# Fixed VectorE and ScalarE order in the first units of each up stage, put-off convolutions, partial products kept in PSUM

## The chip, the cores and the metric

The kernel runs on one core of one Trainium2 chip. The metric is device time in microseconds of one execution, as the median of several runs. TensorE is called PE below, VectorE DVE, ScalarE ACT, and SyncE's queue, which issues nearly all transfers here, SP.

## What is computed

A two-layer trunk over 1024 positions of width 1024, in float32. Layer 0 mixes positions with forgetting attention, layer 1 with a spatial gating MLP (SGU). After each mixer stands the same gated feed-forward block (FFN):

```python
def conv_gated_ffn(h, w_up, conv_w, conv_b, w_down):
    S = h.shape[1]
    a = h @ w_up                                   # 1024 x 1024 @ 1024 x 5632
    ap = jnp.pad(a, ((0, 0), (CONV_WIDTH - 1, 0), (0, 0)))
    acc = ap[:, 0:S] * conv_w[0]
    for j in range(1, CONV_WIDTH):
        acc = acc + ap[:, j:j + S] * conv_w[j]
    a = acc + conv_b
    g, val = jnp.split(a, 2, axis=-1)
    return (jax.nn.silu(g) * val) @ w_down
```

The SGU block begins with `z = gelu(h @ w_in + b_in)`, splits z into u and v, normalises v, mixes it over blocks of 128 positions, and multiplies the result by u ahead of its output product. Each block's input h is `modulate(rmsnorm(x, g), shift, scale)`; shift, scale and the residual's gate come from products of the conditioning vector c with `ada_w`.

## The kernel before

After the attention stage (`fox`) come three pairs of stages, each an `up` and a `down`: FFN of layer 0, SGU, FFN of layer 1. `up` multiplies the block's input by its first weight matrix, `down` the result by the second. Every float32 operand is split in two float32r parts, a rounded copy made by ACT (`put_hi`, line 1133) and the remainder made by DVE (`put_lo`, line 1136, drawn as line 1146 in the profile), and a product is three matmuls (`mm3`).

**Units.** `up` goes unit by unit: 22 in an FFN (128 columns of the gate half and 128 of the value half each), 16 in the SGU. The weights of a unit are two 128x1024 tiles, "g" and "v". Seen as 2x2 blocks, weights A11, A12, A21, A22 times operand blocks B11, B12, B21, B22 take eight block products. From unit 2 on seven products are used instead, by Winograd's form of Strassen's scheme: `p1` A11·B11, `p5` S1·T1, `p6` S2·T2, `p2` A12·B21, `p7` S3·T3, `p3` S4·B22, `p4` A22·T4, in this order. S1 to S4 are sums of weight blocks and T1 to T4 sums of operand blocks. One such product is 12 matmuls of 128x512 (`seven`, four groups of three). Units 0 and 1 are done in the plain form with eight products each, with T1 used in place of B12 (T1 is B12 less B11, so A11·B11 is added back); they need no S, and only B11, B21, T1 and B22. While they run, DVE and ACT have to make T2, T3, T4 and unit 2's sums.

**Units 0 and 1 before.** `half1(u)` makes A11·B11 and A21·B11 in banks a and Y, copies each to the right half R of the unit's output tile in SBUF (line 1386, ACT), and adds A12·B21 and A22·B21 on top (outputs 11 and 21, `post`). `half2` makes A11·T1 + A12·B22 and A21·T1 + A22·B22 in banks X and Y; `post` (line 1645) then adds the copy kept in R by a DVE `tensor_tensor`. The program runs half1(0), half1(1), T1 of both, then B22 of both.

**Weight slots.** The ring `owr` has four tiles of 128x2x1024, the raw weights come to a ring of four tiles `rawr`. In a steady unit, slot 0 takes A11/A12 (`put_a`), slot 1 the A22 of alternate units (`put_w`), slot 2 S3/S1 (`put_v`), slot 3 S2/S4 (`put_g`). `sums_u` makes the S blocks in place in the raw tiles with four DVE operations of 128x512. At the stage's start `start_up` puts g and v of unit 0 in slots 0 and 1, those of unit 1 in 2 and 3, between the last four products of the stage before.

**Operands.** `operands2` makes h in its second half of positions and from it T1, B22, T2, T3, T4. It spills x (four transfers on SP), takes the sum of squares by a matmul with ones, the inverse root on DVE (`norm_t`, `rsqrt`), multiplies a diagonal by ones on PE to spread it, scales x on DVE and ACT (`scale`), and writes the blocks (`put_ops`). `next_operands` hooks it to PE's groups of three matmuls with the numbers 7 and 14: its first part runs once eight groups of the stage have been issued, the rest after fifteen. `operands1` does the same for the first half of positions in the second-last part of `down`, one piece per step.

**After a product.** When both halves of an output are there, `post` in the FFN runs `conv` (line 1632 one ACT activation, line 1634 two DVE `scalar_tensor_tensor` of 128x1023 and 128x1022), SiLU on ACT for the gate half, and for the value half a DVE product; each second unit `store_y` makes four DVE sums and stores to memory. In the SGU, `post` applies GELU, and `natural` (lines 1725 to 1736) transposes v on PE, copies it with ACT, takes `bn_stats` on DVE and stores it.

**What sets the order.** PE's matmuls are chained by hand in program order (`mm`, `strict`). On the other engines a planner simulates the program and puts the instructions in an order by readiness; only between instructions chained by `vo` (DVE) or `ao` (ACT), while `ordered` is true, program order is kept. Before, `ordered` is true inside `operands2` alone. Each engine then runs its queue in that order. SP's queue is in order too: an issue that waits for a free tile holds those behind it.

**Other work in the stages.** `after(f)` of an FFN runs jobs of products with `ada_w` (line 262 four loads into the `rawr` ring, lines 270 and 272 eight DVE operations of 128x512): in the first FFN after units 4, 7, 10, 13, 16, 19. After unit 12, `sgu_tables` prepares tables for the SGU through the same ring.

Of the kernel before, what the change touches and what calls it, by code (L numbers as in the profile page):

```python
# [67 lines left out]
class Trunk:  # L68
# [1151 lines left out]
    def operands1(self, scales):  # L1220
# [7 lines left out]
        yield  # L1228
        next(n, None)
# [8 lines left out]
    def operands2(self, scales):  # L1238
        self.spill(1)
        self.xr.i = -1  # L1240
        self.ordered = True
        n = self.norm_t(1, *scales)
        next(n)
        self.ordered = False
        yield
        self.ordered = True
# [17 lines left out]
        self.put_ops("T2", [t2[:, k] for k in range(4)], second)  # L1264
        self.put_ops("T3", [h[:, L] for h in h2], lambda k: sub(h2[k][:, L], h2[k][:, R], h2[k][:, L]))
        for k in range(4):
            sub(h1[k][:, R], h1[k][:, R], t2[:, k])
        self.put_ops("T4", [h[:, R] for h in h1])
        self.ordered = False
# [26 lines left out]
    def sums_u(self, u):  # L1296
# [4 lines left out]
        self.tt(v[:, lo], g[:, lo], v[:, lo], ALU.subtract)  # L1301
        self.tt(g[:, lo], v[:, hi], g[:, lo], ALU.subtract)
        self.tt(g[:, hi], g[:, hi], g[:, lo], ALU.subtract)

# [30 lines left out]
    def up(self, n, src, post, after):  # L1335
# [45 lines left out]
        def half1(u):  # L1381
            a, x, y = bk[u]
            t = self.out_tiles(u)
            for c, (b, o) in enumerate(((a, "A11"), (y, "A21"))):
                self.seven(b, w[u][o], "B11", True)
                nc.scalar.copy(t[c][:, R], b)
            for b, o, q in ((a, "A12", "11"), (y, "A22", "21")):
                self.seven(b, w[u][o], "B21", False)
                post(u, q, b)

        def half2(u, o, j):
            a, x, y = bk[u]
            t = self.out_tiles(u)
            for c, b in enumerate((x, y)):
                self.seven(b, w[u][f"A{c + 1}{j}"], o, j == 1)
# [535 lines left out]
```

## Time and profile before

| | us |
|---|---|
| median of 3 runs | 2684.41 |
| lowest, highest | 2682.55, 2685.11 |
| the profiled execution | 2688.12 |
| its span, first to last instruction | 2686.3 |
| first up stage, first product | starts at 823.89 |
| SGU's up stage, first product | starts at 1487.02 |
| second FFN's up stage, first product | starts at 2012.73 |

The profiled execution took 1.8 us more than its span, and 3.7 us more than the median of the runs. A timeline row gives start, duration, engine, line, operation, output and inputs, the count of like instructions merged, and in brackets how long the engine had been idle before and which instruction ended that. A row of windows gives, for each engine, busy time and count in the stretch, then the TensorE clock granted (1.00 is full), the share of the DMA engines and the rate.

### The profile page before, as it was taken

To read this page: it belongs to the slowest core of one execution; us is meant where nothing else is said; L and a number is where in the kernel's file an instruction comes from. 1 tells how busy PE (TensorE), PEld (TensorE's weight loads), DVE (VectorE), ACT (ScalarE), POOL (GpSimd) and SP (SyncE) were. 2 spreads that over 40 slices of the span, in tenths; PEclk is the share of its full clock that TensorE was granted. 3 is DMA by queue.
4 is the path that set the end of the run, shared out by engine and by line. 5 is a ranking of instruction groups with operands and counts; after the bars stand their busy time and mean duration, and the time that the engine had idled before them with its cause. 6 is when DMAs were issued, how large, how long until landed. Compare 5 with 4: busy or idle time off the path is not lost.

```text
span 2686.3 us, 35378 instructions
## 1 busy us (share of the span) xinstructions
PE 2573.0 (96%) x12578; PEld 2186.3 (81%) x12578; DVE 2078.6 (77%) x3609; ACT 1463.1 (54%) x2321; POOL 171.5 (6%) x289
## 2 busy tenths in 40 slices
PE   6999999998989899999999999999998999999997
PEld 5988988898878788788888788888876888888886
DVE  7678777888667888888678766766888788877875
ACT  6347666777555545455446644654465545455444
POOL 1122222222100000000000000000000000000000
PEclk8999999999999999999999999999999999999999
DMA  7751111113232344546755346557552243337562
GB/s 232 232 185 56 56 52 56 56 52 99 89 105 74 121 131 140 182 141 200 244 160 171 105 153 190 190 181 275 159 177 72 96 148 116 118 104 286 158 200 91
DMA packets 316521, 379.46 MB, mean 141 GB/s; under 512 B 18872, under 2 KB 196152, under 8 KB 316344
## 3 DMA queue, kind: packets, MB, share of 16 engines
q1 hardware_dynamic: 316120, 377.14, 43.5%
q8 instruction: 99, 1.62, 0.3%
q14 instruction: 78, 0.64, 0.1%
q10 hardware_dynamic: 224, 0.06, 0.0%
HBM read 287.41 MB, written 89.72 MB: 140 GB/s over the span
## 4 chain that ended last, share of the span: by engine, by line
PE 78%; DVE 11%; ACT 4%; DMA 3%; issue 2%; SPq 1%; POOL 0%; DVEq 0%; ACTq 0%; POOLq 0%
PE bankX L104 20%; PE banka L104 17%; PE bankY L104 17%; PE pj L104 7%; PE ms L104 5%; PE o L104 3%; PE s L104 2%; PE ms L157 2%; PE op L104 2%; PE pv L104 1%; DVE ow L1146 1%; DVE hc L1146 1%; PE ms L1755 1%; DVE x L1146 1%; DVE x L1634 1%
## 5 line engine op out<-in xcount | busy, mean ns | idle before, releaser
L1133 ACT CAST ow<-rw 128x1024 fp32r<-128x1024 f32 (+1 forms) x438 | 398.7, 911 | 467.7 <-PE bankY L104 150.4
L1146 DVE TENSOR_TENSOR ow<-rw,ow 128x1024 fp32r<-128x1024 f32 (+1 forms) x438 | 457.0, 1045 | 173.9 <-ACT ow L1133 173.4
L104 PE MATMUL bankX<-hc,ow 128*128 128x512 f32 x1920 | 471.3, 394 | 18.5 <-DVE ow L1146 10.3
L104 PEld LDWEIGHTS bankX<-hc,ow 128*128 128x128 f32 x1920 | 361.1, 189 | 96.5 <-DVE ow L1146 11.9
L104 PE MATMUL banka<-hc,ow 128*128 128x512 f32 x1608 | 391.3, 392 | 1.7 <-DVE ow L1146 1.5
L104 PE MATMUL bankY<-hc,ow 128*128 128x512 f32 x1584 | 387.9, 391 | 0.8 <-DVE ow L1146 0.8
L104 PEld LDWEIGHTS banka<-hc,ow 128*128 128x128 f32 x1608 | 300.4, 188 | 64.4 <-DVE ow L1146 1.8
L104 PEld LDWEIGHTS bankY<-hc,ow 128*128 128x128 f32 x1584 | 296.1, 188 | 64.1 <-issue 1.9
L104 PE MATMUL pj<-x,h 128*128 128x384 f32 (+1 forms) x1536 | 316.6, 348 | 0.2 <-DVE x L119 0.2
L104 PEld LDWEIGHTS pj<-x,h 128*128 128x128 f32 x1536 | 272.6, 193 | 5.0 <-DVE x L119 0.5
L1634 DVE SCALAR_TENSOR_TENSOR x<-x,prm,x 128x1023 f32<-128x1023 f32 (+1 forms) x160 | 204.2, 1279 | 2.7 <-ACT x L1632 2.1
L104 PE MATMUL bankY<-ow 128*128 128x512 f32 x720 | 203.3, 390 | 0.2 <-DVE x L1150 0.2
L104 PE MATMUL banka<-ow 128*128 128x512 f32 x672 | 187.3, 391 | 0.5 <-DVE x L1150 0.5
L104 PEld LDWEIGHTS bankY<-ow 128*128 128x128 f32 x720 | 134.8, 188 | 28.4 <-DVE x L1150 0.6
L104 PE MATMUL bankX<-ow 128*128 128x512 f32 x588 | 156.1, 391 | 0.7 <-DVE ow L1146 0.5
L104 PEld LDWEIGHTS banka<-ow 128*128 128x128 f32 x672 | 125.8, 188 | 27.3 <-ACT x L1183 0.9
L104 PE MATMUL ms<-ow 128*128 128x512 f32 x546 | 139.9, 390 | 0.9 <-DVE pp L1146 0.9
L104 PE MATMUL pv<-pt,w 128*128 128x256 f32 (+1 forms) x640 | 119.8, 297 | 15.3 <-ACT pt L797 12.0
L119 DVE TENSOR_TENSOR pt<-ms,pt 128x512 fp32r<-128x512 f32 (+1 forms) x160 | 100.2, 632 | 40.3 <-ACT pt L797 38.8
L104 PEld LDWEIGHTS bankX<-ow 128*128 128x128 f32 x588 | 110.1, 188 | 25.0 <-DVE ow L1146 2.0
L104 PEld LDWEIGHTS ms<-ow 128*128 128x128 f32 x546 | 102.0, 188 | 23.7 <-DVE pp L1146 2.9
L797 ACT CAST pt<-ms 128x512 fp32r<-128x512 f32 (+1 forms) x160 | 85.4, 540 | 65.9 <-PE ms L157 55.5
(302 smaller groups left out, 3884.8 us busy)
## 6 DMA issues: line engine op xcount, KB each, us to landing
rw<-yd SPq DMA_DIRECT2D x210, 256.0 KB
rw<-in_ffn_w_up_dram SPq DMA_DIRECT2D x88, 512.0 KB
yd<-pp SPq DMA_DIRECT2D x60, 512.0 KB
rw<-in_ada_w_dram SPq DMA_DIRECT2D x48, 512.0 KB
rw<-in_ffn_w_down_dram SPq DMA_DIRECT2D x88, 256.0 KB
rw<-in_sgu_w_in_dram SPq DMA_DIRECT2D x32, 512.0 KB
yd<-x SPq DMA_DIRECT2D x30, 512.0 KB
fraw<-in_fox_w_in_dram SPq DMA_DIRECT2D x96, 128.0 KB
```

The source lines that it names most:

```text
L104: i = self.nc.tensor.matmul(out, lhsT, rhs, start=start, stop=stop, skip_group_check=self.strict)
L119: return (eng or self.nc.vector).tensor_tensor(lo, full, hi.bitcast(F32), op=ALU.subtract)
L157: i = self.nc.tensor.transpose(ps[: s.shape[1], j * P : (j + 1) * P], s, self.ident)
L797: nc.scalar.copy(pt[:, 0, :nb], ps[:, :nb])
L1133: return self.ao(self.nc.scalar.copy(t[:, 0], src))
L1146: return self.vo(self.nc.vector.tensor_tensor(out, a, b, op=op))
L1634: stt(o[:, j:], a[:, : S - j], w[2 - j], o[:, j:], op0=ALU.mult, op1=ALU.add)
L1755: k = nc.tensor.matmul(px[:, b * P : (b + 1) * P], vn[:, b, c * P : (c + 1) * P], sg[:, 0], start=True, stop=True)
```

## The change

In the three `up` stages:

- Units 0 and 1 are interleaved: A11·B11 of both, A12·B21 of both, then A21·B11 and A22·B21 of both (`first`). The partial product A11·B11 is copied by ACT to bank X and A21·B11 to bank a, where T1 and B22 products are accumulated on top. Outputs 12 and 22 are then complete in PSUM, and `post` copies them with ACT (GELU in the SGU) instead of adding with DVE.
- `start_up` therefore loads both units at once and puts g of both before v of both. Slots 1 and 2 change roles: S3/S1 to 1, A22 to 2.
- `operands2` is cut in four parts. The second ends after T2; T3, the four subtractions and T4 follow between B22 products, each ahead of or behind named weight work. `sums_u` is split into `sums_v` and `sums_g`.
- From the B22 products to the end of unit 3, `ordered` is true, so that DVE's `tt` and `conv` operations and ACT's `put_hi` and scale operations keep program order. ACT's copies, its SiLU and the first operation of `conv` are not chained.
- For units below 4, convolution, SiLU, product and store are put in the list `late`, and run one entry at a time at named points of units 2 to 4. In the SGU, `natural` of units 0 and 1 is put off in the same way.
- The operand hooks' numbers go from 7 and 14 to 3 and 10 in the first FFN (after four and eleven groups), and to 7 and 13 in the two other stages. `operands1` waits one step of `down` more ahead of its spreading matmul.
- The jobs of the first FFN run after units 5, 7, 9, 15, 17, 19.

```diff
     def operands2(self, scales):
         self.spill(1)
...
         self.put_ops("T2", [t2[:, k] for k in range(4)], second)
+        yield
         self.put_ops("T3", [h[:, L] for h in h2], lambda k: sub(h2[k][:, L], h2[k][:, R], h2[k][:, L]))
+        yield
         for k in range(4):
             sub(h1[k][:, R], h1[k][:, R], t2[:, k])
+        yield
         self.put_ops("T4", [h[:, R] for h in h1])
-        self.ordered = False
...
     def put_w(self, u):
-        self.put_u(u, "v", ("A22",), 1, u % 2)
+        self.put_u(u, "v", ("A22",), 2, u % 2)
     def put_v(self, u):
-        self.put_u(u, "v", ("S3", "S1"), 2)
+        self.put_u(u, "v", ("S3", "S1"), 1)
...
+        def first(us, c, j):
+            for u in us:
+                a, x, y = bk[u]
+                b = (a, y)[c]
+                self.out_tiles(u)
+                self.seven(b, w[u][f"A{c + 1}{j}"], ("B11", "B21")[j - 1], j == 1)
+                if j == 1:
+                    nc.scalar.copy((x, a)[c], b)
+                else:
+                    post(u, f"{c + 1}1", b)
+        def half2(u, o, j, cs=(0, 1)):
             a, x, y = bk[u]
+            for c in cs:
+                b = (x, a)[c]
+                self.seven(b, w[u][f"A{c + 1}{j}"], o, False)
                 if j == 2:
-                    post(u, f"{c + 1}2", b, t[c][:, R])
+                    post(u, f"{c + 1}2", b)
-        half1(0)
-        half1(1)
+        self.late = []
+        for c in range(2):
+            for j in (1, 2):
+                first((0, 1), c, j)
         half2(0, "T1", 1)
         half2(1, "T1", 1)
         self.load_u(2)
-        half2(0, "B22", 2)
+        self.ordered = True
+        self.put_w(2)
+        next(self.ops2)
+        half2(0, "B22", 2, (0,))
+        self.sums_v(2)
+        half2(0, "B22", 2, (1,))
         self.put_a(2)
-        self.put_w(2)
-        self.sums_u(2)
+        self.sums_g(2)
+        next(self.ops2)
+        half2(1, "B22", 2, (0,))
+        self.put_v(2)
+        next(self.ops2, None)
+        half2(1, "B22", 2, (1,))
+        self.put_g(2)
+        self.run_late()
         after(0)
-        half2(1, "B22", 2)
-        self.put_v(2)
-        self.put_g(2)
         after(1)
         for u in range(2, n):
-            more = u + 1 < n
+            more, early = u + 1 < n, u < 4
             p1(u)
             if more:
                 self.load_u(u + 1)
                 self.put_w(u + 1)
+            if u == 3:
+                self.run_late()
             p5(u)
+            self.run_late()
             p6(u)
             p2(u)
-            if more:
+            if early:
+                self.sums_v(u + 1)
+                if u == 2:
+                    self.run_late()
+                p7(u)
                 self.put_a(u + 1)
-                self.sums_u(u + 1)
-            p7(u)
-            if more:
+                self.sums_g(u + 1)
+                p3(u)
                 self.put_v(u + 1)
-            p3(u)
-            if more:
+                if u == 3:
+                    self.run_late()
+                p4(u)
                 self.put_g(u + 1)
-            p4(u)
+                if u == 3:
+                    self.run_late()
+                    self.ordered = False
...
     def start_up(self, src, steps):
...
+        self.load_u(1)
+        for c, r, names in ((0, "g", ("A11", "A12")), (1, "v", ("A21", "A22"))):
+            for f in steps[2:] if c else ():
+                f()
+            for u in range(2):
+                if not c:
+                    steps[u]()
+                self.put_u(u, r, names, 2 * c + u)
...
+    def next_operands(self, scales, at=(7, 13)):
...
+            if f < 4:
+                self.late.append(lambda: gate(f, c, t[c]))
             else:
+                gate(f, c, t[c])
...
-                if u < 8:
+                if u < 2:
+                    self.late.append(lambda: natural(u, t))
+                elif u < 8:
                     natural(u, t)
...
-        self.next_operands(scales)
+        self.next_operands(scales, (3, 10))
...
-        self.ffn(0, self.ada_jobs([(1, 0), (1, 1), (1, 2)]), range(4, 22, 3), lazy(1, 1), self.sgu_src)
+        self.ffn(0, self.ada_jobs([(1, 0), (1, 1), (1, 2)]), (5, 7, 9, 15, 17, 19), lazy(1, 1), self.sgu_src)
```

Steady units from 4 on keep the old order, except for the one `run_late` after `p5(4)`.

More of the change, by code (lines that the diff above doesn't have):

```diff
@@ L1301, in sums_u, with sums_g, run_late @@
         self.tt(v[:, lo], g[:, lo], v[:, lo], ALU.subtract)
+    def sums_g(self, u):
+        g, v = self.ups[u]["g"], self.ups[u]["v"]
+        lo, hi = slice(0, 4), slice(4, 8)
         self.tt(g[:, lo], v[:, hi], g[:, lo], ALU.subtract)
         self.tt(g[:, hi], g[:, hi], g[:, lo], ALU.subtract)
+    def run_late(self):
+        if self.late:
+            self.late.pop(0)()
     def put_u(self, u, c, names, at, i=None):
@@ L1379, in p4 @@
             post(u, "21", x)
-        def half1(u):
-            a, x, y = bk[u]
[L1383 to L1395, printed above, removed]
-                if j == 2:
-                    post(u, f"{c + 1}2", b, t[c][:, R])
-        half1(0)
-        half1(1)
+        def first(us, c, j):
[9 more added lines that the diff above has]
+        def half2(u, o, j, cs=(0, 1)):
+            a, x, y = bk[u]
+            for c in cs:
+                b = (x, a)[c]
+                self.seven(b, w[u][f"A{c + 1}{j}"], o, False)
+                if j == 2:
+                    post(u, f"{c + 1}2", b)
[3 more added lines that the diff above has]
+                first((0, 1), c, j)
         half2(0, "T1", 1)
@@ L1418, in up @@
                 self.put_w(u + 1)
+            if u == 3:
+                self.run_late()
             p5(u)
+            self.run_late()
             p6(u)
             p2(u)
-            if more:
+            if early:
[3 more added lines that the diff above has]
+                p7(u)
                 self.put_a(u + 1)
-                self.sums_u(u + 1)
-            p7(u)
-            if more:
+                self.sums_g(u + 1)
+                p3(u)
                 self.put_v(u + 1)
-            p3(u)
-            if more:
+                if u == 3:
+                    self.run_late()
+                p4(u)
                 self.put_g(u + 1)
-            p4(u)
+                if u == 3:
+                    self.run_late()
+                    self.ordered = False
+            else:
+                if more:
+                    self.put_a(u + 1)
+                    self.sums_v(u + 1)
+                    self.sums_g(u + 1)
+                p7(u)
+                if more:
+                    self.put_v(u + 1)
+                p3(u)
+                if more:
+                    self.put_g(u + 1)
+                p4(u)
             after(u)
@@ L1439, in start_up, with step @@
         self.load_u(0)
-        for u in range(2):
-            for c, r, names in ((0, "g", ("A11", "A12")), (1, "v", ("A21", "A22"))):
-                steps[2 * u + c]()
-                if (u, c) == (0, 1):
-                    self.load_u(1)
-                self.put_u(u, r, names, 2 * u + c)
-    def next_operands(self, scales):
-        o = self.operands2(scales)
-        self.hook((7, lambda: next(o)), (14, lambda: [None for _ in o]))
+        self.load_u(1)
[7 more added lines that the diff above has]
+    def next_operands(self, scales, at=(7, 13)):
+        self.ops2 = o = self.operands2(scales)
+        def step():
+            self.ordered = True
+            next(o)
+            self.ordered = False
+        self.hook(*((n, step) for n in at))
     Y = {"B11": 0, "T1": 1, "T2": 2, "T3": 3, "T4": 4, "B21": 5, "B22": 6}
@@ L1633, in conv, with gate @@
             for j in (1, 2):
-                stt(o[:, j:], a[:, : S - j], w[2 - j], o[:, j:], op0=ALU.mult, op1=ALU.add)
+                self.vo(stt(o[:, j:], a[:, : S - j], w[2 - j], o[:, j:], op0=ALU.mult, op1=ALU.add))
             return o
+        def gate(f, c, a):
+            ys[f, c] = y = conv(f + c * NF, a)
+            if c == 0:
+                nc.scalar.activation(y, y, AF.Silu)
+            else:
+                y0 = ys[f, 0]
+                self.tt(y0, y0, y, ALU.mult)
+                if f % 2:
+                    self.store_y(yd, f // 2, ys[f - 1, 0], y0)
         def post(f, q, ps, more=None):
```

13 lines of the change are left out of this document (2 added, 11 removed).

## The prediction

> **What bounds the kernel now.** I read the page's head first, then PE's waits, then windows around the gaps.
>
> ```profile
> span 2686.3 us, 35378 instructions
> PE 2573.0 (96%) x12578; PEld 2186.3 (81%) x12578; DVE 2078.6 (77%) x3609; ACT 1463.1 (54%) x2321; POOL 171.5 (6%) x289
> PE bankX L104 <- DVE ow L1146: 10.7, 4, 4.7
> PE bankX L104 <- ACT ow L1133: 7.8, 2, 3.9
> PE ms L104 <- DVE tm L1146: 2.5, 1, 2.5
> 869.26:900.23 30.97, 22.43 (x86) 17.22 (x84) 29.32 (x36) 15.25 (x19) 0.00 (x0) 0.83 0.32 108
> 900.23:919.27 19.04, 19.04 (x86) 15.77 (x84) 14.74 (x17) 9.92 (x13) 0.00 (x0) 1.00 0.14 46
> 1534.20:1558.90 24.70, 22.50 (x110) 18.22 (x109) 19.21 (x34) 13.21 (x21) 0.00 (x0) 1.00 0.32 107
> 2058.80:2090.60 31.80, 22.78 (x86) 17.62 (x85) 29.36 (x36) 15.28 (x19) 0.00 (x0) 0.84 0.32 105
> ```
>
> PE is the bound: 113 us idle in the whole span, and few long waits, all for weight tiles (`ow`). The windows (columns PE, PEld, DVE, ACT, POOL, clock, DMA) are unit 2 and unit 3 of the first FFN, unit 2 of the SGU, unit 2 of the second FFN. A steady unit takes 19.04 us at full clock; unit 2 takes 30.97 and 31.80 in the FFNs, with DVE busy over 29 us of it. There, and only there, DVE is the bound.
>
> ```profile
> 823.89 2.88 PE L104 MATMUL banka<-hc,ow 128*128 128x512 f32 x12
> 826.61 2.88 PE L104 MATMUL bankY<-hc,ow 128*128 128x512 f32 x12
> 869.26 2.88 PE L104 MATMUL banka<-hc,ow 128*128 128x512 f32 x12
> 873.00 2.56 PE L104 MATMUL bankY<-hc,ow 128*128 128x512 f32 x10 [0.40 <-DVE ow L1146]
> 879.47 1.22 PE L104 MATMUL bankX<-hc,ow 128*128 128x512 f32 x2 [3.91 <-ACT ow L1133]
> 884.91 4.58 PE L104 MATMUL bankX<-hc,ow 128*128 128x512 f32 x10 [4.22 <-DVE ow L1146]
> ```
>
> A product starts every 2.72 us. In unit 2, `p5` waits 0.40 us for S1, `p6` 3.91 for the high and 4.22 for the low part of S2: 8.53 us idle. The ten matmuls after it then take 4.58 us, twice their steady 10 x 0.227 = 2.27, and the granted clock is 0.83 in this window. So the gap costs 30.97 - 19.04 = 11.93 us, not 8.53.
>
> **What stands ahead of S2.** DVE's timeline in the first FFN, with the first and the last convolution operations before S2's remainder (six in all), ACT's cast of S2, and S2's remainder in the second FFN:
>
> ```profile
> 836.10 2.48 DVE L1146 TENSOR_TENSOR x<-x,ms 128x512 f32<-128x512 f32 x4 [2.64 <-PE ms L104]
> 865.72 1.27 DVE L1634 SCALAR_TENSOR_TENSOR x<-pp,prm,x 128x1023 f32<-128x1023 f32 x1
> 881.26 2.47 DVE L1634 SCALAR_TENSOR_TENSOR x<-pp,prm,x 128x1022 f32<-128x1022 f32 x2
> 883.65 1.21 DVE L1146 TENSOR_TENSOR ow<-rw,ow 128x1024 fp32r<-128x1024 f32 x1
> 878.37 1.05 ACT L1133 CAST ow<-rw 128x1024 fp32r<-128x1024 f32 x1 [0.50 <-DVE rw L1146]
> 2058.82 2.88 PE L104 MATMUL banka<-hc,ow 128*128 128x512 f32 x12
> 2073.20 1.22 DVE L1146 TENSOR_TENSOR ow<-rw,ow 128x1024 fp32r<-128x1024 f32 x1
> L1146 DVE TENSOR_TENSOR pp<-bankX,pp 128x512 f32<-128x512 f32 x2 | 1.4, 681 | 0.0
> L1146 DVE TENSOR_TENSOR pp<-bankY,pp 128x512 f32<-128x512 f32 x2 | 1.4, 680 | 0.0
> ```
>
> In a row DVE operations of 128x512 take 0.61 us each (2.48 / 4), convolution operations 1.2, 128x1024 about 1.15. The change takes from ahead of S2's end at 884.86:
> - six convolution operations, put off: 6 x 1.2 = 7.2 us;
> - the four additions of kept partial products (the two group rows), now ACT copies: 4 x 0.6 = 2.4;
> - three operations for unit 3 (A22's remainder, two sums) that the planner had let pass: 3 x 0.6 = 1.8. In program order they stand behind.
>
> That is 11.4 us. The operand hook comes one product earlier in the first FFN (four groups, 2.72 us), and by one group, 0.68 us, in the two other stages. By DVE's work S2 is ready at 884.86 - 11.4 - 2.7 = 870.8; the slot is free only when unit 1's last product ends at 869.26, so ACT's cast (1.05) and the remainder (1.21) give about 871.6. PE wants it at 869.26 + 2 x 2.72 = 874.7: 3.1 us to spare. Second FFN: 2074.42 - 11.4 - 0.7 = 2062.3 against 2058.82 + 5.44 = 2064.3: 2.0 to spare. S1 stands before S2 and has the same margin or more. So I take both stalls as gone: **11.9 us** and 31.8 - 19.04 = **12.7 us** (the fourth window's edges, its last digit rounded).
>
> The first part's matmul may now come too soon for its input:
>
> ```profile
> 825.60 0.69 DVE L1146 TENSOR_TENSOR tm<-tm,pp 128x512 f32<-128x512 f32 x1 [0.76 <-ACT pp L888]
> 832.76 0.69 DVE L1146 TENSOR_TENSOR tm<-ident,rs_y 128x512 f32<-128x512 f32 x1
> 835.04 1.02 PE L104 MATMUL ms<-tm,ones 128*128 128x512 f32 x2
> 1493.11 1.02 PE L104 MATMUL ms<-ones,hc 128*128 128x1 f32 x8 [0.49 <-DVE hc L1146]
> ```
>
> Its sum ends at 826.29 and PE would come at 826.61: 0 to 0.5 us of wait, as in the SGU's row; I take 0.3. The diagonal then follows 2.7 us sooner, at 830.7, for a matmul due at 832.2: no wait. The hook moves its four spill issues on SP with it, ahead of `load_u(2)`, whose tiles are wanted 25 us later; I give that nothing.
>
> **What is added.** Four ACT copies per stage, and four partial products now written to PSUM instead of SBUF:
>
> ```profile
> 833.20 0.59 ACT L1642 COPY pp<-banka 128x512 f32<-128x512 f32 x1 [3.09 <-PE banka L104]
> 872.18 0.57 ACT L1348 COPY bankX<-banka 128x512 f32<-128x512 f32 x1 [0.40 <-PE banka L104]
> ```
>
> 0.6 us each, on an engine that sat idle 3.09 us before such a copy. PE may continue a bank once the copy has read it; with two units in turn that is one product, 2.72 us, later. Cover: that other unit's product. Without it, about 1 us per copy. Cost taken: 0, bound 4 us over the three stages.
>
> The put-off work does not vanish: eight convolution operations (9.6), two products (2.3) and a store's sums (2.4) per FFN, 14.3 us, go into units 2 to 4, and unit 2's and 3's own convolutions are shifted too. A steady unit needs 14.74 of 19.04 us of DVE. I walked the fixed order through unit 3, from its start: the addition for output 22 can't begin before `p7` ends, 5 x 2.72 = 13.6; then 0.6 (it), 1.15 (A11/A12), 1.2 (sums), the other addition after 16.32, 1.15 (S3/S1), the gate 2.4 + 1.2, 1.15 (S2/S4): 23.1. Unit 4's `p6` wants it at 19.04 + 5.44 = 24.5. The margin is 1.4 us; earlier units have more. I charge 0.5 us per FFN, bounds 0 to 4.
>
> **SGU, down and the tables.**
>
> ```profile
> 1539.01 0.66 PE L157 MATMUL ms<-ident,pp 128*128 128x128 f32 x4 [0.66 <-ACT x L1733]
> 1545.33 2.60 PE L104 MATMUL banka<-hc,ow 128*128 128x512 f32 x10 [1.54 <-DVE ow L1146]
> 1542.09 2.05 DVE L1735 BATCH_NORM_STATS2 bns<-x 128x6 f32<-128x256 f32 x6
> 1975.62 0.73 PE L104 MATMUL bankX<-ow 128*128 128x512 f32 x2 [0.46 <-DVE ow L1146]
> 1990.00 1.12 PE L104 MATMUL ms<-tm,ones 128*128 128x512 f32 x2 [2.48 <-DVE tm L1146]
> 1112.95 3.06 PE L104 MATMUL bankX<-hc,ow 128*128 128x512 f32 x12 [0.25 <-DVE x L1146]
> 1123.28 2.56 PE L104 MATMUL bankX<-hc,ow 128*128 128x512 f32 x10 [1.34 <-DVE ow L1146]
> ```
>
> SGU: the same S2 wait is 1.54 us, a wait for a transpose bank 0.66. Statistics rows like the third (2.05 / 6 = 0.34 each), the additions and the hook go from ahead of S2, over 6 us against 1.54. The transposes are only moved, and can meet the same two banks: 2.2 less 0.5, **1.7 us**.
>
> SGU's `down`: the spreading matmul waits 2.48 us for DVE. One step later (2.72 us) it finds its input. But PE then reaches the next steps 2.5 us sooner, while DVE is busy, and such a step has waited 0.46 already. Bounds 0 and 2.5; I take **1.8**.
>
> Tables: the waits of 0.25 and 1.34 us come where the jobs after units 10 and 13 and the tables after 12 share DVE and the ring. With jobs after 9 and 15 I count **1.6**, bounds 0 and 1.6.
>
> **Sum.** 11.9 + 12.7 + 1.7 + 1.8 + 1.6 = 29.7; less 0.3 and 2 x 0.5: 28.4 us. The profiled execution of 2688.1 would become 2659.7; it lies 3.7 us over the median, so the median goes to **2656 us**, 1.06% down.
>
> [...]
>
> ```profile
> 1975.00:2000.00 25.00, 22.07 (x98) 1.00 0.34 107
> ```
>
> The rows first: after 4.22 us idle the matmuls took twice their time, after 2.48 us they did not (granted clock 1.00 in this window). [...]
>
> **Rivals.**
> 1. *The gap shrinks but stays*: 2 to 6 us per FFN at S2 of unit 2 or at unit 4, or SGU and `down` give nothing. For it: margins of 2.0 and 1.4 us rest on summed durations, and ACT's waits in between are not all seen. Against: S2 has 11.4 us removed for 4.2 + 3.9 of wait. 2660 to 2676, say 2667.
> 2. *The order binds nothing*: a first operation of `conv` and SiLU are unchained and ACT sends S2's high part as late as now, or the waits move to units 3 to 5 whole. Then only `down` and the tables give: within 0.2%, 2681.
> 3. *Slower: heads of the queue*. DVE has 29.3 us of work in the FFNs' unit 2 window, PE 19.04. If the missing 10.3 us comes up in units 3 and 4 and there each of the four additions for outputs 22 and 12 holds the queue for the product it waits for (2.72 us each, 10.9), with the weights behind it, an FFN loses 21 plus 3 of clock, against 11.9 and 12.7 before: + 24 us, less the 5 of the other parts: 2703. It decides once the margin of 1.4 us at unit 4 is used up. Against: the walk above has these holds in it, and the steady unit leaves 4.3 us. [...]
>
> **Chances.** Forecast (2650 to 2660) 0.60; rival 1 0.23; rival 2 0.07; rival 3 0.06; still lower, if the moved order also takes the 0.49 us waits and small gaps, 0.04. The range 2649 to 2675 holds the first two but for their edges. Faster than 2679 (0.2%, about what a measurement of this kernel tells from no change): 0.87; within: 0.07; slower: 0.06.
>
> **What would show it.** In the changed profile: no wait for `ow` over 0.5 us in unit 2 of the FFNs and clock 1.00 there; four `pp<-bank` additions fewer per stage; S2's remainder right after T4's; no 2.48 us before the spreading matmul. If DVE stands idle ahead of an addition in unit 3 and PE waits for `ow` soon after, rival 3 is right. I am wrong if ACT's chained casts, held by a slot, delay the copies that PE waits for.

## The result and the profile after

The changed kernel takes 2660.3 us (median of 4 runs, 2659.02 to 2661.71), beside 2683.48 for the kernel before in the same runs: a ratio of 0.9914, 95% interval 0.9896 to 0.9931, 23.2 us less. Its profiled execution took 2661.71 us, 26.4 less than that of before.

The head of the page of the changed kernel:

```profile
span 2659.8 us, 35372 instructions
PE 2565.9 (96%) x12578; PEld 2184.4 (82%) x12578; DVE 2072.6 (78%) x3597; ACT 1464.6 (55%) x2329; POOL 170.0 (6%) x289
```

PE has the same 12578 matmuls, DVE has 12 operations fewer (3597 for 3609): the four additions of kept partial products in each of three up stages. PE's idle time fell from 113 us to 2659.8 - 2565.9 = 94 us.

Where the time went is read from one window per stage, from its first product to that of the next stage. The windows of PE alone in the kernel before (us, PE's busy time and count, clock, DMA share, GB/s), in the order first FFN up and down, SGU up and down, second FFN up:

```profile
823.89:1273.13 449.24, 438.97 (x1943) 0.99 0.43 137
1273.13:1487.02 213.89, 212.93 (x937) 1.00 0.60 194
1487.02:1853.15 366.13, 361.50 (x1795) 1.00 0.54 175
1853.15:2012.73 159.58, 156.12 (x685) 1.00 0.57 184
2012.73:2454.24 441.51, 432.00 (x1899) 0.99 0.37 120
```

The same windows of the changed kernel:

```profile
821.66:1256.76 435.10, 434.96 (x1944) 1.00 0.44 141
1256.76:1472.77 216.01, 213.27 (x937) 1.00 0.58 192
1472.77:1838.93 366.16, 362.59 (x1796) 1.00 0.54 175
1838.93:1994.47 155.54, 155.24 (x686) 1.00 0.58 187
1994.47:2427.61 433.14, 430.51 (x1899) 1.00 0.38 123
```

The differences are -14.1, +2.1, 0.0, -4.0 and -8.4 us. The first window also starts 2.2 us sooner. That is not counted as a gain: between two profiles of the changed kernel itself this start differs by 3.6 us (821.66 here, 825.30 in the profile taken again below). What follows the last window differs by less than 0.1. So 24.4 us net were gained in the stages of the change: 22.5 in the `up` stages of the two FFNs and 4.0 in SGU's `down`, while the first FFN's `down` became 2.1 longer.

Windows of the changed kernel on unit 2 of the first FFN and on unit 2 of the second (columns as in the prediction's first fence):

```profile
867.04:886.08 19.04, 19.04 (x86) 15.77 (x84) 18.73 (x22) 13.56 (x18) 0.00 (x0) 1.00 0.23 69
2043.45:2063.91 20.46, 19.63 (x85) 15.61 (x84) 20.14 (x24) 14.11 (x19) 0.00 (x0) 1.00 0.21 64
```

Unit 2 of the first FFN, 30.97 us before, now takes the 19.04 of a steady unit, with PE busy all the time at clock 1.00. DVE is busy 18.73 us of these 19.04, so its work is just covered by PE's. The second FFN's unit 2 went from 31.80 to 20.46.

PE's waits in the changed kernel that have to do with these stages (us in total, times, longest):

```profile
PE ms L104 <- DVE hc L1146: 2.3, 2, 1.8
PE banka L104 <- DVE x L1150: 1.9, 2, 1.6
PE banka L104 <- DVE x L1146: 1.3, 1, 1.3
PE bankX L104 <- DVE x L1146: 0.7, 1, 0.7
```

No wait for a weight tile `ow` is left; the two rows of them in the prediction's first fence made 18.5 us. Four smaller ones stand there now: 1.8 us for the squares at the start of the second FFN, 1.6 for an accumulation in the first FFN's `down`, 1.3 for an addition in the SGU, 0.7 for an addition in the second FFN. Part of what the change won went into them.

### The profile page after: what moved, and what is told of

It is laid out like the page before. It is cut to its first block, busy times and chain, and to the rows that moved or that the text cites. A ratio compares the mean times of both kernels' runs of the same rounds, so it can differ in the third digit from the quotient of the medians.

```text
span 2659.8 us, 35372 instructions
## 1 busy us (share of the span) xinstructions
PE 2565.9 (96%) x12578; PEld 2184.4 (82%) x12578; DVE 2072.6 (78%) x3597; ACT 1464.6 (55%) x2329; POOL 170.0 (6%) x289
## 4 chain that ended last, share of the span: by engine, by line
PE 82%; DVE 8%; ACT 5%; DMA 3%; issue 2%; POOL 0%; SPq 0%; DVEq 0%; ACTq 0%; POOLq 0%
PE bankX L104 21%; PE banka L104 19%; PE bankY L104 17%; PE pj L104 7%; PE ms L104 5%; PE o L104 3%; PE ms L157 2%; PE s L104 2%; PE op L104 2%; PE pv L104 1%; PE ms L1815 1%; DVE ow L1146 1%; DVE pt L119 1%; DVE x L1146 1%; ACT pt L797 1%
## 5 line engine op out<-in xcount | busy, mean ns | idle before, releaser
L104 PE MATMUL bankX<-hc,ow 128*128 128x512 f32 x1968 | 477.6, 391 | 1.0 <-DVE x L1146 0.7
L104 PEld LDWEIGHTS bankX<-hc,ow 128*128 128x128 f32 x1968 | 367.6, 188 | 78.6 <-DVE x L1146 1.7
L104 PE MATMUL banka<-hc,ow 128*128 128x512 f32 x1704 | 415.9, 393 | 1.3 <-DVE x L1146 1.3
L104 PEld LDWEIGHTS banka<-hc,ow 128*128 128x128 f32 x1704 | 319.6, 189 | 68.7 <-DVE x L1146 1.6
L104 PE MATMUL bankY<-hc,ow 128*128 128x512 f32 x1440 | 349.6, 391 | 0.0
L104 PEld LDWEIGHTS bankY<-hc,ow 128*128 128x128 f32 x1440 | 269.2, 188 | 55.8 <-issue 0.5
L1688 DVE SCALAR_TENSOR_TENSOR x<-x,prm,x 128x1022 f32<-128x1022 f32 (+1 forms) x160 | 203.9, 1279 | 2.5 <-ACT x L1686 2.0
L104 PE MATMUL pv<-pt,w 128*128 128x256 f32 (+1 forms) x640 | 119.9, 298 | 15.5 <-ACT pt L797 12.2
```

Of the source, the lines that this page charges most:

```text
L104: i = self.nc.tensor.matmul(out, lhsT, rhs, start=start, stop=stop, skip_group_check=self.strict)
L1688: self.vo(stt(o[:, j:], a[:, : S - j], w[2 - j], o[:, j:], op0=ALU.mult, op1=ALU.add))
```

## The experiments

The twelve runs are told by subject. The first four take away the putting off, the wider order, both, and the partial products in PSUM. The next five follow up the new waits, with the changed kernel run again among them. The last three move a hook or look for a better version. Each edit is against the changed kernel, where nothing else is said. All lengths of stages are measured as above, in the profiled execution. The number behind a median is its ratio to the kernel before, with the 95% interval.

**Order kept, convolutions at once.**

```diff
-            if f < 4:
-                self.late.append(lambda: gate(f, c, t[c]))
-            else:
-                gate(f, c, t[c])
+            gate(f, c, t[c])
```

> The changed kernel, but convolutions run at once (the list of put-off work stays empty in the FFNs; the SGU's transposes stay put off). Theory (the gain is DVE work taken from ahead of S2): six or more convolution operations at 1.2 us come back ahead of S2's remainder, 7 to 9.6 us against a margin of 2.3 us in the first FFN and none in the second, so PE waits 5 to 7 us in unit 2 of the first FFN and 7 to 9 in the second, plus 2 to 3 us each of slow clock: first up stage 443 to 446 us (435.1 in the changed kernel, 449.2 before), third 442 to 446 (433.1, 441.5), whole 2677 to 2683. Rival (the fixed order alone gives the gain): both stages stay within 2 us of the changed kernel's, whole 2660.

Measured: 2723.1 us, 1.0137 of before (1.0107 to 1.0166). The first FFN's `up` took 468.3 us, the second's 463.0. This is slower than the kernel before by 37 us and than the changed one by 63, far more than expected. PE's timeline of this run, two of the waits:

```profile
886.79 4.63 PE L104 MATMUL bankX<-hc,ow 128*128 128x512 f32 x10 [6.91 <-DVE ow L1146]
940.00 4.16 PE L104 MATMUL bankX<-hc,ow 128*128 128x512 f32 x10 [5.58 <-DVE ow L1146]
```

And DVE's:

```profile
873.08 2.60 DVE L1688 SCALAR_TENSOR_TENSOR x<-pp,prm,x 128x1023 f32<-128x1023 f32 x2
897.44 0.69 DVE L1146 TENSOR_TENSOR x<-bankX,pp 128x512 f32<-128x512 f32 x1 [8.65 <-PE bankX L104]
921.53 0.69 DVE L1146 TENSOR_TENSOR x<-bankX,pp 128x512 f32<-128x512 f32 x1 [7.71 <-PE bankX L104]
938.72 1.22 DVE L1146 TENSOR_TENSOR ow<-rw,ow 128x1024 fp32r<-128x1024 f32 x1
```

Both engines wait for each other in turn. Convolutions stand ahead of S2 in the fixed order, so PE waits 6.91 us for `ow`. While PE catches up, DVE comes to the addition for unit 2's product and stands idle for 8.65 us, with the next unit's weight work queued behind it. Once released it has its whole backlog to do, the next unit's weights are late, it idles 7.71 us again one unit on, and PE waits 5.58 us at 940.00, right behind the remainder that begins at 938.72. PE's waits in this stage add up to 23.1 us of the 33.2 over the changed kernel; most of the rest is slow clock behind the long ones (ten matmuls in 4.63 us for 2.27).

**Convolutions put off, order only in `operands2`.**

```diff
-        self.ordered = True
+        def ops2():
+            self.ordered = True
+            next(self.ops2, None)
+            self.ordered = False
```

(and `ops2()` where `next(self.ops2)` stands)

> The changed kernel, but chained order only inside the operand generator, as before the change; convolutions still put off. Theory (putting off does it, the order only saves unit 3's three operations of 0.6 us and places the weights): S2 later by 0 to 2 us, first up stage 435 to 437 us, third 433 to 436, whole 2660 to 2664. Rival (the order is what holds the weights in front; without it the planner again lets other work pass): PE waits 4 us or more for ow in unit 2 or 3, up stages 440 and 438 or more, whole 2668 or more.

Measured: 2673.4 us, 0.9952 (0.9936 to 0.9968); the first FFN's `up` 441.0, the second's 439.6. PE's and then DVE's timeline:

```profile
881.02 0.73 PE L104 MATMUL bankX<-hc,ow 128*128 128x512 f32 x2 [1.30 <-ACT ow L1133]
884.43 4.07 PE L104 MATMUL bankX<-hc,ow 128*128 128x512 f32 x10 [2.67 <-DVE ow L1146]
```

```profile
881.97 1.27 DVE L1692 SCALAR_TENSOR_TENSOR x<-pp,prm,x 128x1022 f32<-128x1022 f32 x1
883.16 1.21 DVE L1146 TENSOR_TENSOR ow<-rw,ow 128x1024 fp32r<-128x1024 f32 x1
```

The convolutions come later in the program, and the planner still puts them ahead of S2's remainder at 883.16. The waits for S2 are smaller than before (1.30 + 2.67 for 3.91 + 4.22) and still there. This is what the rival expected.

**Neither.** Both edits together: convolutions at once, order only in `operands2`.

> The changed kernel with neither: convolutions at once, and chained order only inside the operand generator. What is left of the change: units 0 and 1 interleaved, partials in PSUM, operands in parts, hooks, the step more, jobs. Theory (putting off and the order each do little or harm alone, since the order makes whatever is traced first go first): the planner moves things by readiness, the first up stage takes 441 to 449 us and the third 440 to 446, between the run with put-off work and no order (441.0, 439.6) and the kernel before (449.2, 441.5), far under the 468.3 of order without putting off. Rival (convolutions at once are what costs 33 us, order or not): 460 us or more.

Measured: 2670.8 us, 0.9954 (0.9935 to 0.9973); 440.7 and 439.0 us. In the first FFN PE has the two waits of the run before, nearly to the last digit: 1.30 us for ACT's cast of S2 and 2.68 for its remainder. Both stages are a little shorter than was expected, and far from the rival's 460 us.

So the four combinations stand like this (first FFN's `up` / second FFN's `up` / whole kernel, us):

| | order in `operands2` only | order through unit 3 |
|---|---|---|
| convolutions at once | 440.7 / 439.0 / 2670.8 | 468.3 / 463.0 / 2723.1 |
| convolutions put off | 441.0 / 439.6 / 2673.4 | 435.1 / 433.1 / 2660.3 |

Putting off gains nothing by itself. The order by itself costs 24 to 28 us a stage. Both together gain about 6 us a stage over neither. The remaining 449.2 - 440.7 = 8.5 us of the first `up` come from the parts that this run keeps: units 0 and 1 in turn, partial products in PSUM, the earlier hook, `operands2` in pieces, the jobs after other units.

**Partial products in SBUF.**

```diff
-                    nc.scalar.copy((x, a)[c], b)
+                    nc.scalar.copy(self.ct[u, c][:, R], b)
...
-                self.seven(b, w[u][f"A{c + 1}{j}"], o, False)
+                self.seven(b, w[u][f"A{c + 1}{j}"], o, j == 1)
...
-                    post(u, f"{c + 1}2", b)
+                    post(u, f"{c + 1}2", b, self.ct[u, c][:, R])
```

> The changed kernel, but the partial products A11 B11 and A21 B11 of units 0 and 1 are kept in SBUF and added by DVE (GELU then on the sum), as before the change. Theory: four additions of 0.6 us come back ahead of S2, 2.4 us against a margin of 2.3 us in the first FFN: 435 to 436 us there, and 2 to 3 us more in the third stage (435 to 436), which has no margin; whole 2662 to 2664. Rival (PE waits for the copies to PSUM, so that keeping them there costs what it saves): no stage is longer than in the changed kernel, whole 2660 or less.

Measured: 2665.4 us, 0.9922 (0.9893 to 0.9950), an interval that overlaps that of the changed kernel. The stages are 436.9, 216.0, 367.2, 156.7 and 433.8: 1.8 us more in the first FFN's `up`, 1.0 in the SGU's, 0.7 in the second FFN's, each with small waits that the changed kernel lacks (0.32 us for S2 and 0.69 for an addition in the first FFN, 0.84 for S2 in the second, two of 0.29 at transposes in the SGU). The first FFN lost a little more than was expected, the second less. The four additions brought back stand ahead of S2, and the margin nearly covers them; the copies to PSUM cost PE no wait of their own in the changed kernel.

**The kernel before with one more step for the squares.** In `operands1` of the kernel before:

```diff
         yield
         yield
+        yield
         next(n, None)
```

> The kernel before, with only the one step more of down ahead of the spreading matmul (operands1). Theory: the SGU's down stage goes from 159.6 to about 155.5 us (its 2.5 us wait gone), but the first FFN's down from 213.9 to about 216 (the eight scaling products on DVE now fall on the four accumulations that free the banks, 1.6 us and more of wait), and the third up stage waits about 1.8 us instead of 0.5 for the sum of squares. Whole -2 to +1 against before. Rival (the longer down comes from other parts of the change): the first down stage stays at 213.9.

Measured: 2689.2 us, 1.0014 (1.0001 to 1.0026). SGU's `down` became 3.4 us shorter (156.2), the first FFN's `down` 2.1 longer (216.0) and the second FFN's `up` 3.2 longer (444.7). PE's timeline:

```profile
1453.02 0.94 PE L104 MATMUL banka<-ow 128*128 128x512 f32 x3 [1.61 <-DVE x L1150]
2014.35 1.33 PE L104 MATMUL ms<-ones,hc 128*128 128x1 f32 x8 [1.80 <-DVE hc L1146]
```

Both new waits of the changed kernel, 1.6 and 1.8 us, are here without anything else of the change. The step alone moves the wait of 2.48 us to two other places, and is worth nothing.

**The step after the SGU only.**

```diff
-        yield
+        if self.wait:
+            yield
...
+                self.wait = nj == SG
```

> The changed kernel, but the one step more of down ahead of the spreading matmul only in the SGU's down, not in the first FFN's. Theory (the step puts eight scaling products on the four bank-freeing accumulations): the first FFN's down goes back from 216.0 to about 214 us, waits for accumulations there from 2.4 to about 0.7; all else as in the changed kernel; whole -2. Rival (the first down is longer for another reason): stays at 216.

Measured: 2661.0 us, 0.9910 (0.9892 to 0.9929). The first FFN's `down` is back at 213.8, as before the change, SGU's `down` keeps its 155.5. As a whole this can't be told from the changed kernel: a wait of 1.19 us for an addition at the SGU's tables shows in this execution's first `up`, and it is not in that of the changed kernel.

**The squares ahead of the value weights.** In `start_up`, DVE and ACT in program order while the sums of squares and the first value weights are put:

```diff
         for c, r, names in ((0, "g", ("A11", "A12")), (1, "v", ("A21", "A22"))):
+            self.ordered = c == 1
             for f in steps[2:] if c else ():
                 f()
...
+        self.ordered = False
```

> The changed kernel, but while the last two products of the stage before are issued and the v weights of units 0 and 1 are put, DVE and ACT keep program order, so that the sum of squares (four additions) stands ahead of the v weights' remainders (2 x 1.15 us). Theory: the sum is ready 2.3 us sooner, PE's wait of 1.8 us in the third up stage goes, and with it the slow clock after it (18 matmuls in 5.96 us instead of 4.1): third up stage from 433.1 to about 429 us, S2 there ready in time; the SGU's wait of 0.5 goes as well. Rival 1 (the slow clock is chance and not caused by the wait): the wait goes but the stage gains under 2 us. Rival 2 (squares on ACT end the wait): the wait stays.

Measured: 2655.9 us, 0.9891 (0.9870 to 0.9912). The second FFN's `up` is 430.0 instead of 433.1, and the SGU's 363.1 instead of 366.2; no wait for the squares (`hc`) is left in either. In the SGU that wait was only 0.5 us. The rest of its gain is a shorter wait at a job's addition (0.65 us for 1.32) and a faster clock behind another wait, of which the last section tells.

**Both.** The two edits together.

> The changed kernel with both edits (the step more only in the SGU's down; sum of squares ahead of the v weights). Theory: the two add, 2 us in the first down and 4 in the third up stage, 0.5 in the SGU: about 6 us under the changed kernel, ratio to before about 0.989. Rival (what is won is lost again at unit 3 or at the SGU's jobs): 0 to 3 us under it.

Measured: 2653.0 us, 0.9880 (0.9867 to 0.9894); stages 434.9, 213.9, 363.6, 155.5, 429.8. PE's timeline, then DVE's:

```profile
1990.71 0.95 PE L104 MATMUL ms<-ones,hc 128*128 128x1 f32 x8
```

```profile
1987.38 3.06 DVE L1146 TENSOR_TENSOR hc<-hc,hc 128x512 f32<-128x512 f32 x4
1990.36 2.35 DVE L1146 TENSOR_TENSOR ow<-rw,ow 128x1024 fp32r<-128x1024 f32 x2
```

The four sums of squares now run in one go ahead of two weight remainders, and PE comes to its matmul without a wait.

**The changed kernel again,** for comparison with the three runs before.

> The changed kernel once more, on the same chip, as the measure for the run before. Every theory expects 0.991 of before, the first up stage at 435, the third at 433 us, and the wait of 1.8 us with slow clock behind it in the third if that is caused by the schedule and not by chance.

Measured: 2662.2 us, 0.9913 (0.9900 to 0.9926); stages 436.2, 216.0, 365.4, 156.4, 433.1. The wait of 1.80 us is there again. So is one of 1.23 us at the tables, which the first profile of the same kernel did not have. Both edits are 9.2 us better than this, and the two intervals do not meet.

**The first FFN's hook where the other stages have it.**

```diff
-        self.next_operands(scales, (3, 10))
+        self.next_operands(scales, (7, 13))
```

> The changed kernel, but the first FFN's operand hooks at 7 and 13 as in the other stages. Theory: S2's remainder comes about 2 us later against a margin of 2.3 us, PE's wait stays under 0.5 us, first up stage 435 to 436.5. Rival (the earlier hook carries the gain there): a wait of 2 us or more, and 438 us or more.

Measured: 2661.2 us, 0.9916 (0.9892 to 0.9941). The first `up` is 436.1, with one wait of 0.69 us for an addition, none for `ow`, and 3.31 us for `p6` of unit 2 instead of 2.88: the same picture as in the second FFN, whose hook is at (7, 13). The earlier hook is worth about 0.69 + 0.43 = 1.1 us (the stages differ by 1.0).

**Two more edits** on top of both: the put-off gate that runs last in unit 2 goes behind `p7`, and the SGU's jobs come after units 4 to 7 instead of 3 to 6.

```diff
                 self.sums_v(u + 1)
+                p7(u)
                 if u == 2:
                     self.run_late()
-                p7(u)
...
-            {3: 1, 4: 1, 5: 1, 6: 1},
+            {4: 1, 5: 1, 6: 1, 7: 1},
```

> The kernel with both edits, and two more: in unit 2 the put-off convolution of unit 1 runs behind the addition for output 22 instead of ahead of it, and the SGU's jobs run after units 4 to 7 instead of 3 to 6. Theory: the wait of 0.7 us for that addition in the third up stage goes (429.8 to about 429), and the SGU's wait of 0.6 to 1.3 us at unit 4 goes or moves one unit on (363.6 to 362.5 or the same); whole 0 to 2 us under the kernel with both edits. Rival (DVE stands idle until that addition, and weights come late behind it): a new wait for ow in unit 3 of the FFNs, 1 us or more each.

Measured: 2653.2 us, 0.9877 (0.9860 to 0.9895). The wait of 0.7 us for the addition is gone from the second FFN, and one of 0.76 for S2 stands in unit 3 of both FFNs. The work is only moved: behind unit 2 there is no slack for 2.6 us more. The SGU's `up` gained 2.8 us over both edits (360.8 for 363.6): the wait of 1.13 us at a job's addition is gone and the one at its norm is 0.44 us instead of 1.75, together 2.4. The first `up` has the tables' wait again, 1.18 us.

**Both, with the SGU's jobs one unit later** (of the two more edits the second alone).

> The kernel with both edits, and the SGU's jobs after units 4 to 7, without the moved convolution. Theory (the two edits of the run before act apart: the jobs gave the SGU's 2.8 us, the moved convolution only changed one wait of 0.7 us into another): SGU's up stage 360.8, first and third up stage back at 434.9 and 429.8 with the 0.7 us wait for the addition in the third; whole 2 to 4 us under the kernel with both edits, ratio to before about 0.987. Rival (the SGU stage's 2.8 us came from the moved convolution's place in the order, or from chance): 363.6 again.

Measured: 2650.4 us, 0.9871 (0.9844 to 0.9897), the lowest median of all; stages 434.9, 213.9, 360.7, 155.5, 429.8.

Its interval overlaps that of both edits alone; only the SGU's stage, 2.9 us shorter in one profiled execution each, tells them apart.

## Why the prediction was right, and where it was not

The forecast was 28.4 us less, a median of 2656. Measured are 23.2 us less (18.5 to 27.9 by the interval) and 2660.3: inside the range of 2649 to 2675, and a little short of the forecast itself. Its main mechanism held; several of its smaller terms did not.

**S2 was the bound, and the reason it was late was right.** The forecast said that 11.4 us of DVE work leave from ahead of S2, that both stalls of unit 2 go, and that PE would then have 3.1 us to spare. DVE's and PE's timelines of the changed kernel, first FFN:

```profile
868.93 1.22 DVE L1146 TENSOR_TENSOR ow<-rw,ow 128x1024 fp32r<-128x1024 f32 x1
```

```profile
872.48 2.88 PE L104 MATMUL bankX<-hc,ow 128*128 128x512 f32 x12
```

S2's remainder ends at 870.15, the product that needs it starts at 872.48: 2.3 us to spare. Unit 2 gained the 11.9 us forecast. The first `up` gained 14.1 us where the terms for it (11.9 and 1.6, less 0.3 and 0.5) make 12.7. The 0.3 us for the squares and the 0.5 for the put-off work were not lost there: PE has no wait in this stage. The 1.6 for the tables is uncertain: the changed kernel's two profiles have 0 and 1.23 us of wait at that place, so the gain is 0.4 to 1.6 from one execution to the next. What the 8.5 us of the run with neither edit consist of is open: the partial products (1.8 us) and the hook (about 1) were measured only with the order and the putting off in place.

**Rival 1, that the gap shrinks but stays, is true in part.** The median lies on its border with the forecast (2660). The SGU gave nothing, as this rival allowed, and in the second FFN S2 still costs 0.44 us and an addition behind it 0.69. But no stall of several us is left at S2 or at unit 4, and most of what is missing was lost at other places, as told below.

**Rival 2, that the order binds nothing, is false:** without the order the FFN stages are 5.9 and 6.5 us longer, and the planner does again what it did before. **Rival 3, heads of the queue, did not happen in the change, but its mechanism is real:** the run with nothing put off has DVE idle 8.65 and 7.71 us at the very additions that the rival named, and loses 33 us in the first FFN against the changed kernel, where the rival had 24 (21 plus 3). The rival let it begin at unit 4, with the margin of 1.4 us used up; with nothing put off DVE is held in units 2 and 3, and PE waits for weights in units 2, 3 and 4.

**The largest miss is a wait that the sum had at nothing.** The second FFN gained 8.4 us where 12.7 less 0.5 for the put-off work, 12.2, were forecast. The prediction weighed the squares only for the first FFN, whose hook moves ("0 to 0.5 us of wait, as in the SGU's row; I take 0.3"), and let the wait of 0.49 us at the second FFN's start stand as it was. DVE's timeline at its start, in the changed kernel, then PE's:

```profile
1995.92 1.21 DVE L1146 TENSOR_TENSOR ow<-rw,ow 128x1024 fp32r<-128x1024 f32 x1
...
1998.31 1.22 DVE L1146 TENSOR_TENSOR ow<-rw,ow 128x1024 fp32r<-128x1024 f32 x1
1999.45 2.28 DVE L1146 TENSOR_TENSOR hc<-hc,hc 128x512 f32<-128x512 f32 x3
```

```profile
2001.87 1.02 PE L104 MATMUL ms<-ones,hc 128*128 128x1 f32 x8 [1.80 <-DVE hc L1146]
2002.76 5.96 PE L104 MATMUL banka<-hc,ow 128*128 128x512 f32 x18
```

Two remainders of the value weights, which PE needs later, run ahead of the three sums of squares that it needs next; PE waits 1.80 us, and the 18 matmuls behind take 5.96 us. In the run with neither edit, which has the same wait and keeps its clock, they take 4.37 us:

```profile
2003.45 4.37 PE L104 MATMUL banka<-hc,ow 128*128 128x512 f32 x18
```

So 1.6 us more go to the clock. The prediction foresaw that a shorter SGU `down` brings PE sooner to a busy DVE, but looked for the new wait inside that `down`. It came at the next stage: PE is handed over up to 4.0 us sooner to a DVE whose backlog is as long as ever. The kernel before with the one step shows it with nothing else changed; the squares put ahead of the weights take it away, and that stage then gains 441.5 - 430.0 = 11.5 us, close to the forecast.

The sum also took the slow clock behind a wait that is left at nothing. No run shows this term: behind the 2.48 us of the kernel before the clock stayed at 1.00, but the 1.80 us here were followed by a step of 3.41 us at 0.50 (last section), in which the slow matmuls cost the 1.6 us.

**Margins in the second FFN** were forecast at 2.0 us for S2 and 0.5 us of charge for the put-off work. DVE's timeline of the changed kernel there, then PE's:

```profile
2048.38 1.22 DVE L1146 TENSOR_TENSOR ow<-rw,ow 128x1024 fp32r<-128x1024 f32 x1
...
2057.80 2.59 DVE L1688 SCALAR_TENSOR_TENSOR x<-pp,prm,x 128x1023 f32<-128x1023 f32 x2
2060.32 0.69 DVE L1146 TENSOR_TENSOR x<-bankX,pp 128x512 f32<-128x512 f32 x1
```

```profile
2048.89 3.32 PE L104 MATMUL bankX<-hc,ow 128*128 128x512 f32 x12
...
2061.05 3.02 PE L104 MATMUL bankX<-hc,ow 128*128 128x512 f32 x12 [0.69 <-DVE x L1146]
```

S2's remainder ends at 2049.60, after `p6` has begun at 2048.89: the product takes 3.32 us instead of 2.88, the missing 0.44. The late squares are not the reason, for they hold back PE as well as DVE. With both edits, where the squares wait for nothing, DVE's and PE's timelines show the same 0.44:

```profile
2035.71 1.22 DVE L1146 TENSOR_TENSOR ow<-rw,ow 128x1024 fp32r<-128x1024 f32 x1
```

```profile
2036.23 3.32 PE L104 MATMUL bankX<-hc,ow 128*128 128x512 f32 x12
```

What was mis-sized is the time that DVE needs until S2. The forecast had S2 ready at 2062.3, 49.6 us after the stage's first product at 2012.73; with both edits it is ready at 2036.93, 51.7 us after 1985.27, so 2.1 us later. The operations that the forecast takes away are all gone from between these two points: six convolutions, four additions, and the three for unit 3. Two others have come in, one more 128x1024 remainder of the value weights and one more accumulation of SGU's `down`, about 1.8 us in a row; the stage now starts before DVE has done them. In the first FFN S2 is late too, without any operation added: by DVE's work the forecast was 870.8, 46.9 after the stage's start, and the run has 870.15 less 821.66, 48.5. There DVE stands idle for ACT's casts of weights on the way (0.57 and 0.35 us, 0.33 before), which explains a part; the rest was not traced. The first FFN's hook, 2.72 us earlier, covers its delay; the second FFN's does not.

Twelve microseconds on, a put-off convolution at 2057.80 stands ahead of the addition that frees bank X, and PE waits 0.69 us. That is the charge of 0.5, of about the right size, by put-off work in the queue ahead of an addition; the first FFN pays nothing. Together: 1.80 - 0.49 of wait, 1.6 of clock, 0.44 and 0.69 are 4.0 us, less the 0.5 already charged: 3.5 of the miss of 12.2 - 8.4 = 3.8.

**SGU.** Forecast 1.7, measured 0.0. The two waits named (1.54 and 0.66) did go. In their place DVE's and PE's timelines of the changed kernel show a new one:

```profile
1577.01 1.54 DVE L272 SCALAR_TENSOR_TENSOR tm<-rw,cact,tm 128x512 f32<-128x512 f32 x2 [2.78 <-DMA rw<-in_ada_w_dram]
...
1581.63 0.69 DVE L1146 TENSOR_TENSOR x<-banka,pp 128x512 f32<-128x512 f32 x1
```

```profile
1582.37 3.06 PE L104 MATMUL banka<-hc,ow 128*128 128x512 f32 x12 [1.32 <-DVE x L1146]
```

DVE waits 2.78 us for a job's weights from memory, the addition comes late, PE waits 1.32 us. Another 1.7 us went into slow matmuls behind a wait of 1.75 us at the SGU's norm, which both kernels have, and which was followed by a slow clock in the changed kernel and not in the kernel before (last section). These are 3.0 us against 2.2; the 0.8 us that balance them were not traced. With the jobs one unit later the stage takes 360.7: the forecast missed what else hung on the time of those jobs.

**`down`.** The forecast of 1.8 for SGU's `down` met a net of 1.9 over both `down` stages by luck, from two amounts that it did not have. SGU's `down` gained 4.0: PE's idle time there fell from 159.58 - 156.12 = 3.46 us (2.48 and 0.46 among it) to 0.30, and its busy time by 0.9. The first FFN's `down` lost 2.1. PE's timeline of the changed kernel:

```profile
1441.07 0.93 PE L104 MATMUL banka<-ow 128*128 128x512 f32 x3 [1.61 <-DVE x L1150]
```

One step later, `operands1`'s scaling products on DVE run ahead of the accumulations into x, which PE needs to get its banks back. The forecast named a new wait of this kind and placed it in SGU's `down`; it came in the other `down`, where the step had no wait to remove and the sum had no term. The step there is the cause: with the step after the SGU only, the 2.1 us come back.

In sum the terms gave 28.4 us, and the stages 24.4: 1.4 more than forecast in the first FFN's `up`, 3.8 less in the second's, 1.7 less in the SGU's, and 0.1 more in the two `down`. Another 2.2 lie ahead of the first stage in the profiled execution, so the two profiles differ by 26.4, and the medians by 23.2.

One reading was loose: the few long waits were "all for weight tiles", but the third row beside it, 2.5 us for `tm`, is the spreading matmul's, which the sum counts under `down`.

## What to carry to other kernels

Where an engine with a queue in order feeds the bound, take work that is not urgent away from ahead of the urgent work and fix the order, both: the order alone turned waits into held heads of the queue here (DVE idle 8.65 us at one addition, with nothing put off), and the delay alone was undone by a planner that runs what is ready (1.30 and 2.67 us of wait for S2 left). When a stage becomes faster, look at the next seam: the engines that were covered there have the same backlog as ever and less time for it, and the first thing due (here the squares, 1.80 us of wait) must stand ahead of what only has to be done soon. A step moved to remove one wait should be tried alone and at each place where it runs, since it can pay in one and cost as much in another.

## What the runs showed of the hardware

A wait of the same length was followed by slow matmuls in some runs and not in others. The granted clock of these traces changes only at the edges of steps of 3.41 us, and every stretch of half clock from the start of the first `up` to the end of the third lasts one such step or two or three. In the changed kernel these are 1689.99 to 1693.41 and 2004.02 to 2007.43, one step each at 0.50; in the kernel before 879.07 to 889.31 and 2070.32 to 2080.56, three each. Where a wait fell in these steps tells most of what it cost in the profiles below.

The wait for the squares at the second FFN's start is 1.80 us in nine profiles (1.81 in three of them). Windows of PE alone over two steps of the changed kernel (us, PE's busy time and count, clock, DMA share, GB/s):

```profile
2000.61:2004.02 3.41, 2.15 (x14) 1.00 1.05 364
2004.02:2007.43 3.41, 3.41 (x10) 0.50 0.60 186
```

and over three steps of the run with neither edit:

```profile
1998.24:2001.65 3.41, 2.52 (x12) 1.00 1.01 357
2001.65:2005.06 3.41, 2.50 (x15) 1.00 1.06 362
2005.06:2008.47 3.41, 3.41 (x16) 1.00 0.50 150
```

In the changed kernel 1.26 us of the wait lie in one step (3.41 less 2.15), and the next step runs at half clock, 1.7 us lost. In the run with neither edit the same wait is split into 0.89 and 0.91 us over two steps, and the clock stays at 1.00. The edge inside the wait lies 6.14 us behind the stage's first product in the changed kernel (2000.61 - 1994.47) and 6.49 us behind it in the run with neither edit (2001.65 - 1995.16). All nine profiles go this way: in the seven with half clock behind the wait (the changed kernel twice among them, and two steps of it in the kernel before with one more step), at least 1.26 us of the wait lie in one step; in the two without, at most 0.93.

The wait of 1.75 us at the SGU's norm, in twelve profiles, shows that the place is not all. Split over two steps it was not followed by half clock, in five profiles (the kernel before among them, 1.14 us in one step and the rest in the next). Whole in one step it was in five (the changed kernel twice: in its first profile the wait ends at 1689.89, and the step from 1689.99 has clock 0.50) and was not in two. The 2.48 us wait of the kernel before, 0.88 us in one step and 1.59 in the next, cost only itself, at clock 1.00; no wait of 0.7 us or less in these stages was followed by a slower clock (behind the 0.69 us in the changed kernel's second FFN it is 1.00). So a wait of 1.75 to 1.80 us cost either itself or about twice itself. How much idle time in a step is enough, and whether the short matmuls of the sum of squares (128x1) in the same step count as work, no run here separates.
